# Reordering the start of a hybrid SSD and attention layer: where norms, splits and half steps stand in the queues

## The chip, the cores and the metric

One core of one Trainium2 chip runs the whole layer in one launch. The time is device time in microseconds; a kernel's time is the median of several executions, and one further execution is recorded by the profiler.

## The reference

One decoder layer on a sequence of 1024 tokens with 1024 channels, in float32. RMSNorm, one large projection, a chunked Mamba-2 scan and a forgetting attention side by side, a gated merge, an output projection, a second RMSNorm and the residual:

```python
h = _rmsnorm(x, pre_g)
proj = jnp.einsum('bld,de->ble', h, w_in)
z_ssm, xbc, dt_raw, q, k, v, f_raw, z_att, g_ssm, g_att = jnp.split(proj, ...)
...                       # conv, SiLU, chunked scan -> y_ssm; attention in blocks of 128 -> y_att
p_ssm = jnp.einsum('ble,ed->bld', y_ssm, w_branch_ssm)
p_att = jnp.einsum('ble,ed->bld', y_att, w_branch_att)
merged = jax.nn.sigmoid(g_ssm) * p_ssm + jax.nn.sigmoid(g_att) * p_att
out = jnp.einsum('bld,de->ble', merged, w_out)
return x + _rmsnorm(out, post_g)
```

## The kernel before, in words

The projection's weights are worked off in *pairs* of two units of 128 columns. A pair's product with the normed input is done by a fast 2x2 block scheme with seven block products instead of eight. The operands of the input's side are `b11`, `b21`, `-b22` and the differences `t1`, `-t2`, `t3`, `t4`; those of the weights' side are blocks and sums of blocks (`sum`). Every operand is split into a high part, rounded by ScalarE (`AF.Copy` to fp32r), and a low part, the remainder, made by VectorE. A block product is then 12 matmuls of 128x128 by 128x512: high times high, high times low and low times high, for four blocks of the inner dimension. In the trace the input's operands are called `x0` (`b11`), `x1` (`b21`), `x2` (`-b22`), `x3` (`t1`), `x4` (`-t2`), `x5` (`t3`), `x6` (`t4`), with `h` and `l` for the two parts; the weights' are `wop`.

`Stream` holds the list of block products (*steps*) of all pairs. `stream.halves(n)` issues n half steps of six matmuls each. The list begins with pair 0's product 1, pair 1's product 1, then 0's 2, 1's 2, 0's 6, 5, 7, 4, 3, then pair 1's 6, 5, 7. Three steps ahead of a product its weights are split (`prepare`, lines 349 and 350), and as soon as all readers of a weight buffer are listed, the next load of raw weights (line 342) is queued on SP. Products 1, 6, 7 and 4 of a pair add onto one PSUM bank (`pb`); after 1, 6 and 7 ScalarE copies the bank to `s` (`keep`, line 402). Products 5 and 3 add onto another bank (`pc`); between them line 417 subtracts `s` from it to give a result, on which a tanh follows (line 629).

The start of the kernel is written out in one block. Eight tiles `xt` of x, 128 tokens each, are loaded in two halves. `norm_tiles` computes a tile's sum of squares (line 1197 on ScalarE, for tiles 1 and 3 line 1195 on VectorE), its root (1198, ScalarE), the reciprocal (1199, VectorE), and scales the tile: the first half's on VectorE (1201), the second half's on GpSimd (1203). `stream.begin()` loads more weights and splits those of the first three steps. A loop over k transposes the first half (`turned`, TensorE, line 131, tile `pt`), evicts it with the norm's gain (`low`, lines 1228 and 1230) and splits it into `b11` and `b21` (`put`, lines 1213, 1215, 1217). From k = 4 on each round issues a half step.

A second loop, over j, transposes and evicts the second half (`up`, line 1248), adds to `df`, forms the differences `t1` (1254) and `t2` (1257), splits them, issues a half step and forms `t3` and `t4` in place. Behind it `t3`, `t4` and `-b22` are split, four pieces each, with half steps between; `order=pin` keeps a piece behind what stands before it on its engine. Then the next section opens with its constants (`onesr`, `summing`, `cst`, lines 1288 to 1306), whose generator `dt_and_f` issues the transposing products `pt_df` and goes on with half steps between its parts.

The order on an engine's queue is otherwise chosen by a scheduler at build time: it takes what is ready by its own estimate of times, earlier lines first; instructions under `tc.high_priority()` go ahead of others that are ready. `tc.issue_after(ins)` queues what the block issues on `ins`'s engine behind `ins`, without a wait for its result. TensorE's instructions are kept in the order of the text. On the chip each queue runs strictly in order.

Of the kernel before, what the change touches and what calls it, by code (L numbers as in the profile page):

```python
# [11 lines left out]
AF = mybir.ActivationFunctionType  # L12
ALU = mybir.AluOpType
# [5 lines left out]
D = 1024  # L19
NK = D // P  # L20
KH = NK // 2
# [65 lines left out]
def hybrid_layer(ctx: ExitStack, tc, a, out):  # L87

    nc = tc.nc
# [12 lines left out]
    epst = const.tile([P, 1], F32, name="epst")  # L102
# [24 lines left out]
    def mm(*args, **kw):  # L127
        return tc.keep_in_program_order(nc.tensor.matmul(*args, **kw))  # L128

    def turn(out_, in_, idn=ident):  # L130
        return tc.keep_in_program_order(nc.tensor.transpose(out_, in_, idn))  # L131

    def pin(op):
        return tc.keep_in_program_order(op)

    def small(name="th"):
        return gp.tile([P, HALF], F32, tag="th", name=name)
# [14 lines left out]
    def place(pool, name):  # L152
        i = XOPS.index(name)
        return tuple(pool.tile([P, KH, HALF], F32R, tag=f"x{i}{part}", name=f"x{i}{part}") for part in "hl")
# [4 lines left out]
    class Operands:  # L159
# [37 lines left out]
        def differences(self, j, x, other, cols=slice(0, HALF), room=2, third=None):  # L197
# [48 lines left out]

            wait = (None,) * room
            yield from (start, *wait, less("t1", "x", "x", "y"), keep("b22"), *wait)
            yield from (*low("b22"), less("t2", "x", "y", "x"), keep("b11"), *wait)
            yield from (less("t3", "y", "x", "y"), keep(), *low("t3"), *wait[1:], lambda: fetch("b21"), *wait)  # L250
            yield from (less("t4", "x", "x", "y"), keep(), *low("t4"))

# [34 lines left out]
        def put(self, j, **parts):  # L287
            for name, raw in parts.items():
                self.made.add((name, j))
                name = "-" + name if name in ("t2", "b22") else name  # L290
                self.at[name, j] = self.step
                self.split(name, j, raw)
# [27 lines left out]
    class Pair:  # L320
# [78 lines left out]
        def keep(self, ps):  # L399
            s = wp.tile([P, HALF], F32, tag="s", bufs=3, name="s")  # L400
            with tc.high_priority():
                nc.scalar.activation(s, ps, AF.Copy)  # L402
            return s

        def give(self, unit, ch, ps, s=None, how=None):
# [640 lines left out]
    order = [p for ps in by_group for p in ps]  # L1046
# [120 lines left out]
    with tc.tile_pool(name="pro", bufs=1, reuse_waits="tile", side="right") as pro, tc.tile_pool(  # L1167
        name="prop", bufs=1, space=PSUM, reuse_waits="tile", side="right"
    ) as prop:
        wdf = pro.tile([P, NK, 32], F32, name="wdf")  # L1170
        nc.scalar.dma_start(wdf, a["wdf"])
        preg = pro.tile([P, NK], F32, name="preg")
        nc.scalar.dma_start(preg, a["cst"][:, 80:88])
        ss = pro.tile([P, NT], F32, name="ss")
        rstd = pro.tile([P, NT], F32, name="rstd")
        low = pro.tile([P, NK, HALF], F32, name="low")

        df = prop.tile([P, HALF], F32, name="df")

        early = ExitStack()  # L1180
        xe = early.enter_context(tc.tile_pool(name="xe", bufs=1, reuse_waits="tile"))

        def load_tiles(hf):
            tiles = []
            for t in range(4 * hf, 4 * hf + 4):
                xt = (pro if t < 6 else xe).tile([P, D], F32, tag="xt", bufs=6 if t < 6 else 2, name="xt")
                nc.sync.dma_start(xt, a["x"][t * P : (t + 1) * P, :])
                tiles.append(xt)
            return tiles

        def norm_tiles(hf, tiles):
            for t, xt in enumerate(tiles, 4 * hf):
                sqt = small("sqt").bitcast(BF16)
                if t in (1, 3):
                    nc.vector.tensor_tensor_reduce(sqt, xt, xt, 1.0, 0.0, ALU.mult, ALU.add, ss[:, t : t + 1])
                else:
                    nc.scalar.activation(sqt, xt, AF.Square, accum_out=ss[:, t : t + 1])
                nc.scalar.activation(rstd[:, t : t + 1], ss[:, t : t + 1], AF.Sqrt, bias=epst, scale=1.0 / D)
                nc.vector.reciprocal(rstd[:, t : t + 1], rstd[:, t : t + 1])
                if hf == 0:  # L1200
                    nc.vector.tensor_scalar(xt, xt, rstd[:, t : t + 1], None, ALU.mult)
                else:
                    nc.gpsimd.tensor_scalar(xt, xt, rstd[:, t : t + 1], None, ALU.mult)

        def turned(tiles, k):
            pt = prop.tile([P, HALF], F32, tag="pt", bufs=2, name="pt")
            for j in range(4):
                turn(pt[:, j * P : (j + 1) * P], tiles[j][:, k * P : (k + 1) * P]) 
            return pt

        def put(name, j, src, sign=1.0, order=lambda op: op):
            h, l = (p[:, j, :] for p in xop[name])
            made = [order(nc.scalar.activation(h, src, AF.Copy, scale=sign))]
            if sign == 1.0:
                made.append(order(nc.vector.tensor_tensor(l, src, h, ALU.subtract)))
            else:
                made.append(order(nc.vector.scalar_tensor_tensor(l, src, sign, h, ALU.mult, ALU.subtract)))
            return [op.ins for op in made]

        tiles = load_tiles(0)  # L1220
        stream = Stream(order + late + ends, len(order) + 3, len(order) + len(late) + 4)
        norm_tiles(0, tiles)
        tiles2 = load_tiles(1)
        stream.begin()
        for k in range(NK):
            pt = turned(tiles, k)
            if k > 1:
                nc.scalar.activation(low[:, k, :], pt, AF.Copy, scale=preg[:, k : k + 1])
            else:
                nc.vector.tensor_scalar(low[:, k, :], pt, preg[:, k : k + 1], None, ALU.mult)  # L1230
            put("b11" if k < KH else "b21", k % KH, low[:, k, :])
            if k >= KH:
                stream.halves(1)
        norm_tiles(1, tiles2)

        for k, h in [(k, h) for j in range(KH) for k, h in ((j, 0), (j + KH, 0), (j + KH, 1))]:
            pin(nc.sync.dma_start(wo_dram[k, :, half(h)], a["wo"][k * P : (k + 1) * P, half(h)]))

        b22 = []
        for j in range(KH):  # L1240
            up = []
            if j % 2 == 0:
                two = pro.tile([P, D], F32, tag="xt", bufs=6, name="b22")
                b22 += [two[:, 0:HALF], two[:, HALF:D]]
            for k in (j, j + KH):
                pt = turned(tiles2, k)
                up.append(b22[j] if k >= KH else pro.tile([P, HALF], F32, tag="up", bufs=1, name="up"))
                nc.scalar.activation(up[-1], pt, AF.Copy, scale=preg[:, k : k + 1])
            b11, b21 = low[:, j, :], low[:, j + KH, :]
            for n, (k, m) in enumerate(((j, b11), (j, up[0]), (j + KH, b21), (j + KH, up[1]))):  # L1250
                mm(df[32 * n : 32 * n + 32, :], wdf[:, k, :], m, start=(j == 0), stop=(j == KH - 1))
            with tc.high_priority():
                t1 = small()
                nc.vector.tensor_tensor(t1, up[0], b11, ALU.subtract)
                put("t1", j, t1)
                t2 = small()
                nc.vector.tensor_tensor(t2, up[1], t1, ALU.subtract)
                last = put("-t2", j, t2, -1.0)
            stream.halves(1)

            with tc.issue_after(last[1]) if j == KH - 1 else nullcontext():
                nc.vector.tensor_tensor(b11, t2, b11, ALU.subtract)
                nc.vector.tensor_tensor(b21, t2, b21, ALU.subtract)
        dft = small("dft")
        nc.scalar.activation(dft, df, AF.Identity, bias=bdf)
        stream.halves(1)

        with tc.issue_after(last[0]), tc.issue_after(last[1]):
            for j in range(KH):
                put("t3", j, low[:, j, :], order=pin)  # L1270
        stream.halves(1)
        early.close()
        pools["t4"] = phase_a.enter_context(tc.tile_pool(name="xp4", bufs=1, reuse_waits="tile"))
        xop["t4"] = place(pools["t4"], "t4")
        for j in range(KH):
            put("t4", j, low[:, j + KH, :], order=pin)
        stream.halves(1)
        for j in range(KH):
            put("-b22", j, b22[j], -1.0, order=pin)
        stream.halves(5)  # L1280


    with tc.tile_pool(name="ssm", bufs=1, reuse_waits="tile", side="right") as sp, tc.tile_pool(
# [509 lines left out]
```

## Time and profile before

| | us |
|---|---|
| median of 3 runs | 1277.48 (1276.88 to 1279.33) |
| the profiled execution | 1273.87 |
| its span | 1272.2 |
| TensorE busy | 1246.1 (98%) |
| VectorE busy | 1012.9 (80%) |
| ScalarE busy | 794.3 (62%) |
| GpSimd busy | 319.3 (25%) |

A row of the timeline reads: start, duration, engine, line, operation, output<-inputs, shapes, count, and in brackets the idle time before it and what ended that. SPq is SP's queue, on which transfers are issued. A row with a count above 1 merges instructions that follow each other. L349 and L350 are a weight operand's two halves, L1213 with L1215 or L1217 an input operand's. The last instructions of a product overlap with the next, so a product's length is read from the starts.

### The profile page before, as it was taken

How to read it: one execution, taken by the hardware profiler on the slowest of the kernel's cores; microseconds unless marked ns; L12 is line 12 of the kernel's file. 1: busy time of each engine (PE TensorE's matmuls, PEld its weight loads, DVE VectorE, ACT ScalarE, POOL GpSimd, SP SyncE). 2: the span in 40 equal slices, each digit the busy share in tenths (PEclk: the TensorE clock that was granted, in tenths of full speed). 3: DMA queues.
4: the chain of work that ended last, by engine and by line, in shares of the span. 5: the costliest groups of instructions: out<-in, count | busy, mean ns of one | idle time of the engine just before them, and what ended most of it. 6: DMA issues, size and time to landing. Idle time of an engine off the chain costs nothing.

```text
span 1272.2 us, 20822 instructions
## 1 busy us (share of the span) xinstructions
PE 1246.1 (98%) x6926; PEld 982.3 (77%) x6926; DVE 1012.9 (80%) x1994; ACT 794.3 (62%) x1737; POOL 319.3 (25%) x322
## 2 busy tenths in 40 slices
PE   5999999999999999999999999999999999999997
PEld 3678888888888888888887777777777777778886
DVE  7988886988888978997767676767789767886975
ACT  7745665556665765566555666666687666844753
POOL 4000440013400241115102124223112212356062
PEclk9999999999999999999999999999999999999999
DMA  8232452545436533744447576666687657766933
GB/s 300 69 120 76 146 162 88 191 152 182 138 101 215 175 127 117 219 146 140 142 149 252 162 228 212 217 214 218 232 286 263 224 184 249 249 221 199 364 110 105
DMA packets 152236, 233.56 MB, mean 184 GB/s; under 512 B 15201, under 2 KB 60737, under 8 KB 152129
## 3 DMA queue, kind: packets, MB, share of 16 engines
q1 hardware_dynamic: 136064, 196.08, 47.7%
q10 hardware_dynamic: 10560, 18.06, 3.8%
q0 software_dynamic: 5504, 18.09, 3.7%
q8 instruction: 54, 0.88, 0.3%
q14 instruction: 54, 0.43, 0.1%
HBM read 162.99 MB, written 72.34 MB: 185 GB/s over the span
## 4 chain that ended last, share of the span: by engine, by line
PE 86%; DMA 4%; DVE 4%; ACT 4%; issue 1%; SPq 0%; POOL 0%; DVEq 0%; ACTq 0%; POOLq 0%
PE pb L128 36%; PE pc L128 21%; PE pd L128 7%; PE av L128 5%; PE pt L131 5%; PE s L128 5%; PE yps L128 2%; PE st L128 1%; ACT ex L1509 1%; DMA xt<-in_x 1%; PE tr L131 1%; PE tr_v L131 1%; DMA v<-v_dram 1%; PE df L128 1%; DVE wop L350 1%
## 5 line engine op out<-in xcount | busy, mean ns | idle before, releaser
L350 DVE TENSOR_TENSOR wop<-sum,wop 128x512 fp32r<-128x512 f32 x180 | 140.2, 780 | 53.6 <-ACT wop L349 52.6
L349 ACT ACTIVATE wop<-sum 128x512 fp32r<-128x512 f32 x180 | 112.5, 626 | 109.0 <-DVE sum L355 52.4
L1509 ACT ACTIVATE ex<-ex,nm 128x512 f32<-128x512 f32 (+1 forms) x192 | 116.2, 606 | 71.9 <-DVE nm L1505 71.6
L402 ACT ACTIVATE s<-pb 128x512 f32<-128x512 f32 x144 | 85.3, 593 | 98.2 <-PE pb L128 96.2
L128 PE MATMUL pb<-x0h,wop 128*128 128x512 f32 x384 | 131.5, 399 | 0.0
L128 PE MATMUL pb<-x6h,wop 128*128 128x512 f32 x384 | 129.5, 395 | 1.3 <-ACT s L402 1.3
L128 PE MATMUL pb<-x5h,wop 128*128 128x512 f32 x384 | 130.1, 396 | 0.7 <-ACT s L402 0.7
L350 DVE TENSOR_TENSOR wop<-raw,wop 128x512 fp32r<-128x512 f32 x144 | 105.4, 733 | 31.8 <-ACT wop L349 31.5
L128 PE MATMUL pc<-x3h,wop 128*128 128x512 f32 x384 | 129.8, 396 | 0.5 <-DVE ot L419 0.4
L128 PE MATMUL pc<-x2h,wop 128*128 128x512 f32 x384 | 130.2, 397 | 0.0
L128 PE MATMUL pb<-x4h,wop 128*128 128x512 f32 x384 | 129.1, 395 | 0.0
L1505 DVE CUSTOM_DVE_ANT_0 ex<-s,fb 128x512 f32<-128x512 f32 (+1 forms) x192 | 96.8, 552 | 20.0 <-PE s L128 14.8
L349 ACT ACTIVATE wop<-raw 128x512 fp32r<-128x512 f32 x144 | 89.7, 623 | 14.7 <-PE pd L128 6.1
L128 PE MATMUL pd<-x1h,wop 128*128 128x512 f32 x288 | 96.3, 394 | 0.0
L128 PEld LDWEIGHTS pb<-x6h,wop 128*128 128x128 f32 x384 | 72.1, 188 | 18.6 <-issue 2.0
L128 PEld LDWEIGHTS pb<-x5h,wop 128*128 128x128 f32 x384 | 72.1, 188 | 18.4 <-issue 2.0
L128 PEld LDWEIGHTS pb<-x0h,wop 128*128 128x128 f32 x384 | 72.6, 189 | 17.6 <-issue 2.9
L128 PEld LDWEIGHTS pc<-x3h,wop 128*128 128x128 f32 x384 | 72.1, 188 | 17.7 <-issue 1.5
L128 PEld LDWEIGHTS pc<-x2h,wop 128*128 128x128 f32 x384 | 72.1, 188 | 17.4 <-issue 2.4
L128 PEld LDWEIGHTS pb<-x4h,wop 128*128 128x128 f32 x384 | 72.1, 188 | 16.7 <-issue 1.9
L211 POOL TENSOR_TENSOR wd<-wd 128x256 f32<-128x256 f32 x32 | 32.4, 1011 | 205.0 <-DMA wd<-in_wo 135.0
L131 PE MATMUL pt<-ident,ex 128*128 128x128 f32 x576 | 75.1, 273 | 2.0 <-ACT ex L1509 1.4
(318 smaller groups left out, 2993.6 us busy)
## 6 DMA issues: line engine op xcount, KB each, us to landing
raw<-in_wu SPq DMA_DIRECT2D x128, 256.0 KB
csb<-cs_dram SPq DMA_DIRECT2D x32, 256.0 KB
q<-q_dram SPq DMA_DIRECT2D x32, 256.0 KB
k<-k_dram SPq DMA_DIRECT2D x16, 512.0 KB
fb<-f_dram SPq DMA_DIRECT2D x16, 512.0 KB
rb<-st_dram SPq DMA_DIRECT2D x48, 128.0 KB
wd<-in_wo SPq DMA_DIRECT2D x40, 128.0 KB
xt<-in_x SPq DMA_DIRECT2D x8, 512.0 KB
```

What stands on the lines that cost most here:

```text
L128: return tc.keep_in_program_order(nc.tensor.matmul(*args, **kw))
L131: return tc.keep_in_program_order(nc.tensor.transpose(out_, in_, idn))
L211: pin(nc.gpsimd.tensor_tensor(t[out_], t[a_], t[b_], ALU.subtract))
L349: nc.scalar.activation(op[:, 0], src, AF.Copy)
L350: nc.vector.tensor_tensor(op[:, 1], src, op[:, 0], ALU.subtract)
L402: nc.scalar.activation(s, ps, AF.Copy)
L1505: nc.vector.tensor_tensor_reduce(o, s[e][:, 0:w], fb[hp, h][:, e, 0:w], 1.0, 3.0e38, ALU.add, ALU.min, nm)
L1509: pin(nc.scalar.activation(o, o, AF.Exp, scale=-1.0, bias=nm, accum_out=hd.at(hd.sm, i, h, e)))
```

## The change

The first half's norms are issued under high priority, and the splits in `stream.begin()` are queued behind tile 3's root on ScalarE and behind tile 3's scaling on VectorE. Tile 7 is scaled by VectorE instead of GpSimd. In the last round of the second loop `-t2` is split before `t1`. Of the four pieces of `-b22` the last is split two half steps later, behind the copy `s` of pair 0's product 7, and seven half steps instead of five stand between the first pieces of `-b22` and the next section.

```diff
@@ class Pair
         def keep(self, ps):
             s = wp.tile([P, HALF], F32, tag="s", bufs=3, name="s")
             with tc.high_priority():
-                nc.scalar.activation(s, ps, AF.Copy)
+                self.copied = nc.scalar.activation(s, ps, AF.Copy).ins
             return s
@@ norm_tiles
-                nc.scalar.activation(rstd[:, t : t + 1], ss[:, t : t + 1], AF.Sqrt, bias=epst, scale=1.0 / D)
+                root = nc.scalar.activation(rstd[:, t : t + 1], ss[:, t : t + 1], AF.Sqrt, bias=epst, scale=1.0 / D)
                 nc.vector.reciprocal(rstd[:, t : t + 1], rstd[:, t : t + 1])
-                if hf == 0:
-                    nc.vector.tensor_scalar(xt, xt, rstd[:, t : t + 1], None, ALU.mult)
+                if hf == 0 or t == 7:
+                    scaled = nc.vector.tensor_scalar(xt, xt, rstd[:, t : t + 1], None, ALU.mult)
                 else:
                     nc.gpsimd.tensor_scalar(xt, xt, rstd[:, t : t + 1], None, ALU.mult)
+            return root.ins, scaled.ins
@@ the start
-        norm_tiles(0, tiles)
+        with tc.high_priority():
+            root, scaled = norm_tiles(0, tiles)
         tiles2 = load_tiles(1)
-        stream.begin()
+        with tc.issue_after(root), tc.issue_after(scaled):
+            stream.begin()
@@ the second loop
                 nc.vector.tensor_tensor(t1, up[0], b11, ALU.subtract)
-                put("t1", j, t1)
+                if j < KH - 1:
+                    put("t1", j, t1)
                 t2 = small()
                 nc.vector.tensor_tensor(t2, up[1], t1, ALU.subtract)
                 last = put("-t2", j, t2, -1.0)
+                if j == KH - 1:
+                    with tc.issue_after(last[0]), tc.issue_after(last[1]):
+                        put("t1", j, t1)
             stream.halves(1)
@@ behind it
         stream.halves(1)
-        for j in range(KH):
+        for j in range(KH - 1):
             put("-b22", j, b22[j], -1.0, order=pin)
-        stream.halves(5)
+        stream.halves(3)
+        with tc.issue_after(stream.pairs[0].copied):
+            put("-b22", KH - 1, b22[KH - 1], -1.0, order=pin)
+        stream.halves(4)
```

## The prediction

> **What bounds the kernel now.** I read the page first, then the busy time by stretches, then TensorE's waits, then the timelines of the stretches that wait. Beside the page's share for TensorE stand the stretches (columns: span, TensorE, weight load, VectorE, ScalarE, GpSimd busy, then granted clock, DMA share, GB/s).
>
> ```profile
> PE 1246.1 (98%) x6926; PEld 982.3 (77%) x6926; DVE 1012.9 (80%) x1994; ACT 794.3 (62%) x1737; POOL 319.3 (25%) x322
> 0.00:64.00 64.00, 48.43 (x217) 32.50 (x218) 53.51 (x98) 47.68 (x90) 15.02 (x12) 1.00 0.52 185
> 64.00:200.00 136.00, 136.00 (x720) 109.69 (x719) 117.05 (x213) 80.02 (x163) 28.51 (x24) 1.00 0.42 124
> 12.00:29.00 17.00, 14.17 (x65) 10.47 (x66) 14.85 (x23) 16.96 (x35) 12.89 (x4) 1.00 0.91 323
> 29.00:45.40 16.40, 16.40 (x78) 8.69 (x79) 14.96 (x25) 11.04 (x17) 0.00 (x0) 1.00 0.12 41
> 51.50:55.60 4.10, 2.86 (x13) 2.05 (x11) 4.10 (x8) 4.10 (x8) 0.00 (x0) 1.00 0.60 208
> ```
>
> TensorE is idle for 26.1 us of the span, and 15.6 of them lie in the first 64 us. In the next 136 us it never waits. All edits lie in the first 64 us, so what TensorE gains there it should keep: a fully busy TensorE afterwards just runs the same list earlier. The wait list of TensorE there (total us, times, longest) is the budget:
>
> ```profile
> PE pt L131 <- DVE rstd L1199: 8.6, 1, 8.6
> PE pt L131 <- DVE xt L1201: 2.8, 3, 1.5
> PE pt L131 <- ACT low L1228: 1.4, 1, 1.4
> PE pb L128 <- ACT s L402: 1.3, 1, 1.3
> PE pt L131 <- POOL xt L1203: 0.6, 1, 0.6
> PE pt_df L128 <- DVE summing L1304: 0.5, 1, 0.5
> PE pb L128 <- DVE x4l L1217: 0.3, 1, 0.3
> ```
>
> The first is the start-up and stays. Everything else is 6.9 us, 0.54% of the span: an upper end for any gain. But three stretches have another engine full: ScalarE from 12 to 29 (16.96 of 17.00), TensorE from 29 to 45.4, and both VectorE and ScalarE from 51.5 to 55.6 (4.10 of 4.10 each). A wait that is removed in such a stretch comes back as a wait for the full engine. I call pair 0's seven products p1 to p7, pair 1's q1 to q7.
>
> **Part 1: first half's norms ahead of the weights' split.**
>
> ```profile
> 10.06 0.63 ACT L349 ACTIVATE wop<-raw 128x512 fp32r<-128x512 f32 x1 [0.81 <-DMA raw<-in_wu]
> 10.61 0.29 ACT L1198 ACTIVATE rstd<-ss,epst 128x1 f32<-128x1 f32 x1
> 11.16 0.69 DVE L350 TENSOR_TENSOR wop<-raw,wop 128x512 fp32r<-128x512 f32 x1
> 11.76 0.16 DVE L1199 RECIPROCAL rstd<-rstd 128x1 f32<-128x1 f32 x1
> 12.01 1.06 ACT L1197 ACTIVATE sqt<-xt 128x1024 bf16<-128x1024 f32 x1 [1.11 <-DMA xt<-in_x]
> ```
>
> Tile 3's root ends at 10.90, but its reciprocal stands behind the split and runs at 11.76. With the split behind, it can run at 11.16: tile 3, and the transposes that need it, come 0.6 us sooner. The split's ScalarE half moves from 10.06 to about 10.90, still ahead of the 12.01 at which ScalarE becomes full, and is covered by that idle time. What does 0.6 us bring? From 12 to 29 ScalarE has 0.04 us to spare, and its work (squares, evictions, splits) is the same in both kernels, so the stretch ends where it ended. I take 0. Bounds: -0.6 if it all came through, +0.5 if the split's 0.63 us fell into the full stretch. The raw weights' loads stand on SP's queue as before, since the order is imposed on ScalarE and VectorE alone.
>
> **Part 2: the last tile scaled by VectorE.**
>
> ```profile
> 22.98 0.15 DVE L1199 RECIPROCAL rstd<-rstd 128x1 f32<-128x1 f32 x1
> 24.24 2.85 POOL L1203 TENSOR_SCALAR xt<-xt,rstd 128x1024 f32<-128x1024 f32 x1
> 24.66 1.24 DVE L350 TENSOR_TENSOR wop<-sum,wop 128x512 fp32r<-128x512 f32 x1 [0.34 <-ACT wop L349]
> 27.70 0.64 ACT L349 ACTIVATE wop<-sum 128x512 fp32r<-128x512 f32 x1
> 28.22 0.70 ACT L1248 ACTIVATE up<-pt,preg 128x512 f32<-128x512 f32 x1
> 11.95 0.75 DVE L1201 TENSOR_SCALAR xt<-xt,rstd 128x1024 f32<-128x1024 f32 x1
> ```
>
> Tile 7 is ready at 27.09 now (24.24 + 2.85). On VectorE the same operation costs 0.75 us (the row of tile 3), so it could be ready by 23.13 + 0.75 = 23.9, and TensorE's 0.6 us wait goes. What is late next is the eviction `up` at 28.22, behind ScalarE's unbroken queue. Only one thing ahead of it can give way: p5's split at 27.70, which is traced after `up` and went first. If they swap, `up` starts 0.52 us sooner; if not, nothing is won. I take -0.35, bounds 0 and -0.6. VectorE pays 0.75 and gets back some of it: the split at 24.66, begun just after GpSimd's last scaling, took 1.24 instead of 0.69 us. The net of 0.2 us lies beside TensorE's full stretch from 29 to 45.4, in which VectorE has 1.44 us to spare.
>
> The Trainium skill ("SBUF — State Buffer", Who interferes with whom) speaks against this edit: VectorE and GpSimd share a port pair that one of them locks for a whole instruction, and a scaling on VectorE contends for it. By it the scaling would wait from 23.13 to 24.24 for GpSimd's third tile, 1.1 us more; if VectorE's spare time covered none of that, the sum below would be -0.5 instead of -1.6. The stretched split shows a hold of 0.55 us, not one of 2.85, so the trace agrees with a hold but not with its length.
>
> **Part 3: the last piece of -t2 ahead of t1's.**
>
> ```profile
> 46.23 0.69 DVE L1215 TENSOR_TENSOR x3l<-th,x3h 128x512 fp32r<-128x512 f32 x1
> 47.43 0.69 DVE L1217 SCALAR_TENSOR_TENSOR x4l<-th,x4h 128x512 fp32r<-128x512 f32 x1
> 48.17 0.50 PE L128 MATMUL pb<-x4l,wop 128*128 128x512 f32 x1 [0.30 <-DVE x4l L1217]
> ```
>
> VectorE splits t1 at 46.23 and -t2 at 47.43, and p6 waits 0.30 us for the latter. Swapped, x4l is 0.6 us sooner and the wait goes; t1's piece is needed only by p5's last quarter. What is late next is `s` (part 4), which ScalarE's queue sets, so by itself this brings 0. It may cost: t1's ScalarE half can no longer run ahead of -t2's. Bounds -0.3 and +0.5.
>
> **Part 4: the last piece of -b22 behind the copy `s`.**
>
> ```profile
> 53.47 1.68 ACT L1213 ACTIVATE x2h<-b 128x512 fp32r<-128x512 f32 x3
> 55.03 0.59 ACT L402 ACTIVATE s<-pb 128x512 f32<-128x512 f32 x1
> 55.67 0.50 PE L128 MATMUL pb<-x6h,wop 128*128 128x512 f32 x1 [1.31 <-ACT s L402]
> ```
>
> p4 adds onto the bank that `s` copies, so it cannot start before. Three pieces run from 53.47 to 55.03, 0.52 each; with one behind `s`, p4 starts at 55.15. Bounds: 0 (part 3 gives it back) and -1.3 (the whole wait). The moved piece now also stands behind the tanh of the next result on ScalarE, and behind it pair 1's splits: that chain must be done before p3's last quarter.
>
> **Part 5: two more half steps (p3) before the next section.** They bring p3 ahead of the transposes pt_df, and p3's two loads and q7's split ahead of the section's set-up in the text.
>
> ```profile
> 57.06 0.68 DVE L355 TENSOR_TENSOR sum<-sum,raw 128x512 f32<-128x512 f32 x1
> 57.67 0.69 DVE L1217 SCALAR_TENSOR_TENSOR x2l<-b,x2h 128x512 fp32r<-128x512 f32 x1
> 58.27 0.69 DVE L417 TENSOR_TENSOR th<-pc,s 128x512 f32<-128x512 f32 x1
> 59.23 1.10 PE L128 MATMUL pt_df<-summing,dft 128*128 128x64 f32 x8 [0.53 <-DVE summing L1304]
> 60.14 0.48 PE L128 MATMUL pc<-x2h,wop 128*128 128x512 f32 x1
> 62.97 0.69 DVE L350 TENSOR_TENSOR wop<-sum,wop 128x512 fp32r<-128x512 f32 x1 [0.37 <-ACT wop L349]
> 62.98 0.39 PE L128 MATMUL pb<-x4h,wop 128*128 128x512 f32 x1
> 53.12 0.42 SPq L1296 DMA_DIRECT2D cst<-in_cst  x1
> 61.30 0.33 SPq L342 DMA_DIRECT2D raw<-in_wu  x1
> 63.14 2.72 PE pb L128 x12
> ```
>
> A product takes 2.72 us (the chain's row), pt_df 0.91 (59.23 to 60.14). With parts 2 and 4, p4 runs from 54.8 to 57.5. p3 may follow at once, without the 0.53 us for `summing`, but it writes the bank that the subtraction at 58.27 reads, so that is late next. It loses one 0.60 us piece ahead of it (57.67) and gains part 2's 0.35: 57.3 to 58.0. If the sum at 57.06 also falls behind it, it ends at 57.4 and p4's end, 57.5, decides. So p3 starts between 57.5 and 58.0, and q6, which starts at 62.98 now, between 57.5 + 2.72 + 0.91 = 61.1 and 61.6: a gain of 1.4 to 1.9. On SP's queue p3's loads (61.30, when their buffers come free) are now traced ahead of the constants `cst` (53.12). Nothing ties `cst` to them, so I take 0; issued right behind them it would be 8.5 us late, and its first readers, on VectorE and ScalarE, would wait: that belongs to the backlog below. After q6 the order is the old one. I take the middle, **-1.6 us for all parts together**.
>
> The profiled execution took 1273.87 us, of which 1272.2 are the span; it would become 1272.3. The median shown, 1277.48, is 3.6 above it, so the work is a difference: 1277.48 - 1.6 = **1275.9 us**. One measurement can tell about 0.2%, 2.6 us, from no change; my forecast is inside.
>
> **Rivals.**
> *Free queues (-3.1).* An earlier start makes the schedule put `s` and the subtraction at 58.27 ahead of more pieces than the last one. Then p4 starts without the 1.3 and 0.3 us: 55.67 - 1.6 - 0.5 = 53.6, and p4, p3, pt_df run on: q6 at 59.9. For it: both are marked urgent, and part 3 makes p7 end sooner. Against: VectorE and ScalarE are full there. It gives 1274.4.
>
> *Backlog on VectorE (+1.4).* `summing` is now traced after q6's, q5's and q7's splits, on an engine that is full. If it falls behind q7's split (62.97 + 0.69, less 0.35), pt_df runs from 63.4 and q6 starts at 64.4: 1278.9. It decides as soon as `summing` is later than p3's end, 60.7; each further operation ahead of it costs 0.6, so two more bring +2.6, and a late `cst` more. Against: before, `summing` found a gap ahead of those splits, and can again.
>
> *Nothing (0).* ScalarE's order stays, part 3 eats part 4, and `summing` stalls p3's successor as it stalled p3: 1277.5.
>
> **How the numbers follow.** Forecast 0.43, free queues 0.34, backlog 0.18 (0.14 of it beyond +2.6, since an overfull VectorE tends to hold several operations), nothing 0.05. Faster by over 0.2%: free queues and the forecast's lower edge, 0.35. Within: 0.42 + 0.05 + 0.04 = 0.51. Slower: 0.14. The range goes from 1273.3 (free queues, less 1.1, about half of the 2.45 us over which the three runs of before spread) to 1279.0 (backlog as priced); beyond it I leave 0.2.
>
> **What would show it.** Right: tile 7's scaling on VectorE near 0.75 us with no wait of TensorE for GpSimd; no wait for x4l; `s` directly after three pieces of x2h; p3 right behind p4 and pt_df behind p3 without a wait; q6 at 61.1 to 61.6; no new wait of TensorE from 64 to 600. Wrong: `up` still behind p5's split, a new wait of pt_df for `summing` or of p3 for x2l, or waits that appear past 64 us, where nothing was edited.

## The result and the profile after

The changed kernel took 1280.18 us (median of 19 executions, 1278.09 the lowest) against 1276.88 us for the kernel before (19 executions, beside it on the same chips). The ratio is 1.0028, with a 95% interval of 1.0020 to 1.0036: by the ratio 3.6 us slower, where 1.6 us faster was forecast. One execution of the changed kernel took 3399 us; like single ones of 2067 and 6167 us in later runs, it is left out of the ratios. The profiled execution of after took 1278.09 us, its span 1276.4. First its busy shares and stretches, with the columns as in the prediction:

```profile
PE 1247.9 (98%) x6926; PEld 982.7 (77%) x6926; DVE 1012.1 (79%) x1995; ACT 795.8 (62%) x1738; POOL 312.1 (24%) x321
```

```profile
0.00:64.00 64.00, 47.25 (x201) 30.08 (x201) 49.76 (x88) 46.99 (x87) 9.57 (x9) 1.00 0.48 171
29.00:45.40 16.40, 14.32 (x66) 7.20 (x66) 13.00 (x21) 9.78 (x17) 0.00 (x0) 1.00 0.14 47
```

TensorE did the same 6926 matmuls, but 201 instead of 217 of them in the first 64 us. ScalarE has one instruction more (1738). The stretch from 29 to 45.4, in which TensorE never waited before, now has 2.1 us of idle time. TensorE's waits (total us, times, longest) from 0 to 64 and, in the last two rows, from 64 to 200:

```profile
PE pt L131 <- DVE rstd L1199: 9.0, 1, 9.0
...
PE pb L128 <- ACT s L402: 1.9, 1, 1.9
PE df L128 <- ACT b L1251: 1.5, 1, 1.5
PE pb L128 <- DVE x0l L1216: 0.9, 1, 0.9
...
PE df L128 <- ACT up L1251: 0.6, 1, 0.6
...
PE pc L128 <- ACT x2h L1214: 0.3, 1, 0.3
PE pc L128 <- DVE x2l L1218: 0.2, 1, 0.2
```

The three waits that parts 2, 3 and 5 aimed at are gone: GpSimd's tile (0.6), `x4l` (0.3), `summing` (0.5). In their place stand `b` (1.5), `x0l` (0.9), `up` (0.6), a longer `s` (1.9 for 1.3), `x2h` and `x2l`.

From the timelines of both kernels I take, for one and the same matmul, how much later it starts after the change; I call this its *lag*. The first transpose has +0.39, the first matmul on `up` (28.97 before) +0.67, the fifth such matmul (37.95) +1.20, the second matmul of the next product, p6, (45.66) +3.16, p4 +3.15, q6 +3.39. From there up to 670 us it stays within 0.3 us, for matmuls that keep their place in the order. One 0.8 us wait for a result of line 415 at 675 us and small drifts bring it to +4.2 at the end, which is the difference of the two profiled executions (1278.09 - 1273.87). So most of the loss, 2.5 of 3.4 us, was made between 28 and 45 us, where the change edits nothing.

### The profile page after: what moved, and what is told of

Same layout as the page of the kernel before. It is cut to its first block, busy times and chain, and to the rows that moved or that the text cites. A ratio compares the mean times of both kernels' runs of the same rounds, so it can differ in the third digit from the quotient of the medians.

```text
span 1276.4 us, 20823 instructions
## 1 busy us (share of the span) xinstructions
PE 1247.9 (98%) x6926; PEld 982.7 (77%) x6926; DVE 1012.1 (79%) x1995; ACT 795.8 (62%) x1738; POOL 312.1 (24%) x321
## 4 chain that ended last, share of the span: by engine, by line
PE 84%; DVE 5%; ACT 5%; DMA 4%; issue 1%; SPq 0%; POOL 0%; DVEq 0%; ACTq 0%; POOLq 0%
PE pb L128 36%; PE pc L128 21%; PE pd L128 7%; PE av L128 4%; PE s L128 4%; PE pt L131 4%; PE yps L128 2%; ACT ex L1519 1%; PE st L128 1%; PE tr L131 1%; PE tr_v L131 1%; DVE ex L1515 1%; DVE wop L350 1%; PE tr L128 1%; ACT wop L349 1%
```

## The experiments

Each run stood beside the kernel before on one chip, with 12 executions (6 of two_behind and all_mended). "q6" is the lag of q6's first matmul (62.98 us before) in the profiled execution. The last column turns the ratio into time at 1276.9 us.

| run | ratio, 95% | q6, us | time, us |
|---|---|---|---|
| the whole change | 1.0028 [1.0020, 1.0036] | +3.39 | +3.6 |
| part1_alone | 1.0004 [0.9993, 1.0015] | +1.51 | +0.5 |
| part2_alone | 1.0025 [1.0013, 1.0037] | +2.68 | +3.2 |
| part3_alone | 1.0005 [0.9995, 1.0016] | +1.42 | +0.6 |
| part45_alone | 1.0024 [1.0005, 1.0043] | +1.53 | +3.1 |
| part2_tanh_behind | 1.0003 [0.9992, 1.0014] | +0.67 | +0.4 |
| after_tanh_behind | 1.0012 [1.0003, 1.0022] | +1.39 | +1.5 |
| part45_unpinned | 0.9991 [0.9982, 1.0000] | +0.15 | -1.1 |
| after_no_priority | 1.0025 [1.0011, 1.0039] | +2.97 | +3.2 |
| part5_alone | 1.0000 [0.9989, 1.0010] | -0.45 | 0.0 |
| two_behind | 1.0049 [1.0032, 1.0066] | -1.91 | +6.3 |
| all_mended | 1.0050 [1.0033, 1.0067] | -1.05 | +6.4 |
| four_mended | 1.0005 [0.9993, 1.0017] | -0.08 | +0.6 |

Two cautions for this table. The times of the parts alone add up to 7.4 us and not to 3.6, so no part's share of the loss can be read from it as it stands. And the times hold something that "q6" does not: the granted clock, the share of its full speed that TensorE was given, as the mean over an execution. Where 62 executions of the kernel before had a clock of 0.999, they took 1275.6 us on average; seven with 0.997 took 1279.4. The mean clock was 0.9985 to 0.9987 for the kernel before, 0.9972 in part3_alone, 0.9970 in part45_alone, 0.9962 in all_mended and 0.9957 in two_behind. As an estimate, 0.001 of some 1277 us is 1.3 us, so that about 2 us of part45_alone's +3.1 lie there, more than 3 us in all_mended and almost 4 us of two_behind's +6.3. The main loss is not of that kind: among executions with 0.999 the whole change took 1279.5 us on average (seven) and part2_alone 1278.8 (five), against the 1275.6 of before.

My theory after the result was that each part costs by the order it gives to *other* work in the engines' queues. The main rival was that the edited operations themselves cost: the scaling on VectorE, or the crowded VectorE that the prediction's backlog describes.

**Part 2 alone, and with the tanh tied.**

```diff
-                if hf == 0:
+                if hf == 0 or t == 7:
```

> The kernel before with part 2 alone: tile 7 scaled by VectorE. Theory (queue order): the tanh of pair 0's first result, with its table load of 1.28 us, goes ahead of the second eviction `b` in the third round of the second loop; TensorE waits about 1.5 us for `b` where it waited for nothing, and everything behind it is 2.0 to 2.5 us later: q6 near 65.2, total +2.2. Rival 1 (port lock): the scaling on VectorE takes 1.8 us or more instead of 0.75, and that is the loss: total 0 to +0.5, tanh where it was. Rival 2 (the prediction): -0.35.

The largest loss of a part alone is here: +3.2 us for a single condition. ScalarE in the third round of the second loop, first before, then the whole change:

```profile
37.23 0.67 ACT L1248 ACTIVATE up<-pt,preg 128x512 f32<-128x512 f32 x1
37.80 0.68 ACT L1248 ACTIVATE b<-pt,preg 128x512 f32<-128x512 f32 x1
38.50 1.28 ACT L629 ACT_TABLE_LOAD   x1
39.79 0.63 ACT L629 ACTIVATE th<-th 128x512 f32<-128x512 f32 x1
```

```profile
24.97 0.74 DVE L1201 TENSOR_SCALAR xt<-xt,rstd 128x1024 f32<-128x1024 f32 x1
28.39 0.62 ACT L349 ACTIVATE wop<-sum 128x512 fp32r<-128x512 f32 x1
28.91 0.68 ACT L1251 ACTIVATE up<-pt,preg 128x512 f32<-128x512 f32 x1
...
37.92 0.61 ACT L1214 ACTIVATE x4h<-th 128x512 fp32r<-128x512 f32 x1
38.44 0.67 ACT L1251 ACTIVATE up<-pt,preg 128x512 f32<-128x512 f32 x1
39.12 1.28 ACT L629 ACT_TABLE_LOAD   x1
40.42 0.63 ACT L629 ACTIVATE th<-th 128x512 f32<-128x512 f32 x1
40.95 0.67 ACT L1251 ACTIVATE b<-pt,preg 128x512 f32<-128x512 f32 x1
...
41.68 1.05 PE L128 MATMUL df<-b,wdf 128*32 128x512 f32 x2 [1.47 <-ACT b L1251]
```

Before, `b` stands ahead of the first tanh and of the table load that it brings. After, the order is `x4h`, `up`, table load, tanh, `b`. The table load and the tanh's 0.53 us step (40.42 to 40.95) put 1.8 us ahead of `b`, and TensorE waits 1.47 us for it. part2_alone has the same order (`up` 37.94, table load 38.63, tanh 39.92, `b` 40.46) and the same wait. Why the scheduler chose this order, no run shows. The scaling itself did what the prediction said, 0.74 us on VectorE; in part2_alone it took 1.03. In the next run the tanh is tied behind `b`:

```diff
-            nc.scalar.activation(t[ch], t[ch], AF.Tanh, scale=0.5)
+            def go(order=None):
+                with tc.issue_after(order) if order else nullcontext():
+                    nc.scalar.activation(t[ch], t[ch], AF.Tanh, scale=0.5)
...
+            if stream.count < 6:
+                stream.after(2, lambda: go(stream.evicted))
```

> Part 2 alone, and in addition the tanh of pair 0's first result queued behind the eviction `b` of the third round (nothing else moved). Theory (the loss of part 2 is that queue order): TensorE's wait of 1.5 us for `b` goes, the second loop runs as before, and the lag at q6 falls from 2.6 us to 0.7 us or less; time against before between -0.5 and +0.8 us, where part 2 alone had +3.2. Rival 1 (the loss is the scaling on VectorE itself, by the port it shares with GpSimd): lag at q6 stays at 2 us or more. Rival 2 (the loss lies behind the first 64 us): the wait goes and the time stays at +2.5.

The wait for `b` is gone, and the time is back to 1.0003. The same tie in the whole change:

> The changed kernel whole, and in addition the tanh queued behind the eviction `b`. Theory: the largest single loss goes, lag at q6 from 3.4 to about 1.0 to 1.5 us (what is left is the first table load, the later `s` and the wait for x2h); time against before +0.5 to +1.5 us, ratio near 1.0008, where the change had 1.0028. Rival (the other three parts cost as much by themselves, the sum of the single lags at q6 being 7 us and not 3.4): the time stays at +2.5 or more.

It took 2.0 us off the lag of q6 (3.39 to 1.39) and 2.0 us off the time (+3.6 to +1.5, rounded). This order is the largest single term, shown by taking it out twice.

**Part 1 alone, and the whole change without its priority.** The first has only the priority and the two `issue_after`; the second leaves out `with tc.high_priority()` and keeps the rest.

> The kernel before with part 1 alone: the first half's norms under high priority, the first splits behind tile 3's root and scaling. Theory (a changed queue order costs more than the freed wait): high priority lets the first Square go ahead of the warm-up Sqrt, so ScalarE loads two tables (2 x 1.28 us) where it loaded one; the first transpose comes 0.4 us later, `up` of the second loop 0.5 to 0.7 us later, and pair 1's product 6 (q6, 62.98 before) starts near 63.6: total +0.6. Rival 1 (the prediction: ScalarE is full from 12 to 29, so nothing moves): 0 within 0.3. Rival 2 (the loss of the whole change sits behind the first 64 us): 0 at q6 and a new wait of TensorE later.

> The changed kernel whole, without the high priority around the first half's norms (the split still stands behind tile 3's root and scaling). Theory: ScalarE loads one table at the start again, the first transpose is 0.4 us earlier than in the changed kernel, but the order of squares and evictions behind it is the same, so `up` and all behind it are 0.1 to 0.4 us earlier: ratio to before 1.0025. Rival (the extra table load is the main loss): ratio 1.0010 or less.

ScalarE's start after the whole change:

```profile
2.19 1.28 ACT L1197 ACT_TABLE_LOAD   x1 [2.19 <-issue]
...
6.14 1.28 ACT L105 ACT_TABLE_LOAD   x1
```

The priority let the first square go ahead of the warm-up root, so a function of another table came first, and ScalarE loads two tables instead of one. The Trainium skill ("ScalarE: Activation LUTs", Table sets: the hidden batching unit) says that tables are loaded as sets of functions, and that going from a function of one set to one of another takes a load each time. The trace agrees: here the second load, 1.28 us, came in with the new order. Without the priority there is one load, and the first transpose has a lag of -0.08 instead of +0.39. But q6 changed only from +3.39 to +2.97, and the time (1.0025 against 1.0028) can't tell. part1_alone shows a lag of +1.51, with waits for `x0l` (1.2) and `x0h` (0.8), since squares and evictions changed places on the full ScalarE. But part of this lag is not the order's: behind these waits TensorE ran at half clock from 22.5 to 25.9 us, which it did not in the profile of the whole change (granted clock third from the end):

```profile
24.00:26.00 2.00, 2.00 (x7) 1.61 (x7) 2.00 (x4) 1.97 (x5) 1.68 (x1) 0.52 0.82 281
```

Its time of 1.0004 holds both that and nothing. So the extra load is shown in the trace; its share of the time stays unsettled.

**Part 3 alone.**

```diff
+                if j < KH - 1:
+                    put("t1", j, t1)
...
+                if j == KH - 1:
+                    with tc.issue_after(last[0]), tc.issue_after(last[1]):
+                        put("t1", j, t1)
```

> The kernel before with part 3 alone: the last piece of -t2 split ahead of t1's. Theory (queue order): the wait of 0.3 us for x4l goes, p5 and p7 start 0.5 us sooner, but the copy `s` now stands behind dft and the last piece of x6h on ScalarE, so p4 starts where it did or 0.2 us later: total 0 to +0.2. Rival (the wait was all there was): p4 and all behind it 0.3 to 0.5 us sooner, total -0.4.

The wait for `x4l` went, and the wait for `s` grew from 1.31 to 2.38. p7 ended 0.46 us sooner, and `s` came 0.62 us later (55.65 for 55.03); I had expected p4 at most 0.2 us later, and its lag grew by 0.5. My expectation blamed `dft` and the last `x6h`, but both stood ahead of this `s` before too (`dft` at 48.76). ScalarE has no gap from 45.7 up to `s`, and only one instruction there is new: `t1`'s half `x3h`. Before, it ran at 43.45, ahead of a gap; now it takes 0.52 us of the full stretch. So here the cost is the moved piece's own place, and not an order given to other work. First before, then part3_alone:

```profile
43.45 0.63 ACT L1213 ACTIVATE x3h<-th 128x512 fp32r<-128x512 f32 x1
45.62 0.63 ACT L349 ACTIVATE wop<-raw 128x512 fp32r<-128x512 f32 x1 [1.54 <-PE pd L128]
```

```profile
46.77 0.61 ACT L1213 ACTIVATE x3h<-th 128x512 fp32r<-128x512 f32 x1
...
54.56 0.68 ACT L1269 ACTIVATE dft<-df,bdf 128x512 f32<-128x512 f32 x1
...
55.65 0.58 ACT L402 ACTIVATE s<-pb 128x512 f32<-128x512 f32 x1
...
56.29 0.50 PE L128 MATMUL pb<-x6h,wop 128*128 128x512 f32 x1 [2.38 <-ACT s L402]
```

The whole change shows the same thing. `x3h` stands in the full stretch, at 49.85, and takes the place that part 4 freed, so that part 4's gain is gone:

```profile
49.85 0.61 ACT L1214 ACTIVATE x3h<-th 128x512 fp32r<-128x512 f32 x1
...
55.54 1.67 ACT L1214 ACTIVATE x2h<-b 128x512 fp32r<-128x512 f32 x3
...
58.20 0.57 ACT L402 ACTIVATE s<-pb 128x512 f32<-128x512 f32 x1
58.83 0.50 PE L128 MATMUL pb<-x6h,wop 128*128 128x512 f32 x1 [1.86 <-ACT s L402]
...
61.01 1.15 ACT L349 ACTIVATE wop<-sum 128x512 fp32r<-128x512 f32 x2 [2.24 <-DVE sum L355]
61.70 0.43 PE L128 MATMUL pc<-x2h,wop 128*128 128x512 f32 x1
...
62.07 0.58 ACT L413 ACTIVATE th<-pb 128x512 f32<-128x512 f32 x1
62.55 1.14 ACT L629 ACTIVATE th<-th 128x512 f32<-128x512 f32 x2
63.59 0.62 ACT L1214 ACTIVATE x2h<-b 128x512 fp32r<-128x512 f32 x1
...
64.26 0.50 PE L128 MATMUL pc<-x2h,wop 128*128 128x512 f32 x1 [0.28 <-ACT x2h L1214]
```

The same rows show part 5's price. p3 starts right behind p4 at 61.70, as meant, but its last quarter needs the moved piece of `x2h`. That stands pinned behind two splits, a copy and two tanh and runs at 63.59. With its low part and the two waits p3 takes 3.86 us (61.70 to pt_df at 65.56) instead of the 2.72 of the prediction.

**Parts 4 and 5 alone, pinned and not pinned.**

```diff
-        for j in range(KH):
+        for j in range(KH - 1):
...
+        with tc.issue_after(stream.pairs[0].copied):
+            put("-b22", KH - 1, b22[KH - 1], -1.0, order=pin)
```

> The kernel before with parts 4 and 5 alone: the last piece of -b22 behind the copy `s`, and two more half steps ahead of the next section. Theory (queue order): `s` is 0.5 us sooner and p4 with it; p3 follows p4 at once, but the last x2h stands behind the tanh and two weight splits on ScalarE, so p3 waits 0.5 to 1.0 us in its last quarter; q6 0.5 us sooner (62.5), total -0.5. Rival 1 (the prediction's parts 4 and 5 without part 2): q6 1.0 to 1.5 us sooner, total -1.3. Rival 2 (constants queued behind weight loads on SP stall VectorE and TensorE later): +0.8 or more, with the wait past 64 us.

> Parts 4 and 5 alone, but the last piece of -b22 tied only to the copy `s` and no longer to what stands ahead of it in the text, so that it runs on ScalarE right behind `s`, ahead of the tanh and the weights' splits. Theory (p3's waits of 1.2 and 0.2 us come from that place in the queue): both go, p3 runs through, and q6 starts 1.0 to 2.0 us earlier than before instead of 1.5 later; time against before -1.0 to -2.0 us. Rival (the constants queued behind weight loads on SP are the loss of parts 4 and 5): the waits for x2h go and the time is still above before by 1 us or more.

Pinned, `s` came 0.45 us sooner, as the prediction has it, and p3 then waited 1.2 us for `x2h` and 0.2 for `x2l`: q6 at +1.53, where I had expected -0.5. Its time of +3.1 is more than this order, since about 2 us go with the lower clock; its three executions with a clock of 0.999 took 1275.5 us on average, no more than before. Whether the order brought the lower clock stays open. In the second run only `order=pin` of the last piece is left out. ScalarE then takes that piece right behind `s`:

```profile
55.53 0.58 ACT L402 ACTIVATE s<-pb 128x512 f32<-128x512 f32 x1
56.01 0.63 ACT L1213 ACTIVATE x2h<-b 128x512 fp32r<-128x512 f32 x1
```

p3's waits for `x2h` and `x2l` are gone. Its q6 lag of +0.15 includes +1.0 us that it already had at 28.97 us, ahead of all that was edited (matmuls start 0.43 us apart up to 23.6 us there, up to 20.2 us before), so the edit itself brought about -0.9; I had expected -1.0 to -2.0. Its time, 0.9991 [0.9982, 1.0000], is the only one of these runs with an interval that does not reach above 1, and that only just. It is the best version found, some 1.1 us below before and, by the two ratios, 4.7 us below the change.

**Part 5 alone**: `halves(7)` for `halves(5)`, all four pieces ahead of `s`.

> Part 5 alone: seven half steps instead of five behind the pieces of -b22, all four of which stay ahead of the copy `s`. Theory (the waits for x2h come from the moved piece, not from the moved half steps): no wait for x2h or x2l; p4 starts as before (wait for `s` 1.3 us), p3 follows within 0.4 us of p4's end once the subtraction of L417 is done, pt_df has no wait; q6 0.5 to 0.9 us earlier than before; time -0.3 to -1.0 us. Rival (the constants, queued behind weight loads on SP, stall VectorE and ScalarE): time above before by 0.5 us or more, with a wait of TensorE past 64 us.

q6 comes 0.45 us sooner and the time is 1.0000, where I had expected a gain of 0.3 to 1.0 us. In its profile later waits of 1.5 us for `x3l`, 0.6 for line 417 and 0.5 for line 415 took the place of what was won.

**Two pieces and `dft` behind `s`, without parts 1 and 2, and then with all five parts.**

```diff
-        nc.scalar.activation(dft, df, AF.Identity, bias=bdf)
...
+        with tc.issue_after(stream.pairs[0].copied):
+            nc.scalar.activation(dft, df, AF.Identity, bias=bdf)
+            for j in range(KH - 2, KH):
+                put("-b22", j, b22[j], -1.0)
```

> Parts 3, 4 and 5 with the orders mended: -t2 ahead of t1, two pieces of -b22 (not one) and dft behind the copy `s`, tied to `s` alone; part 1 and part 2 left out. Theory (each wait comes from what stands ahead on ScalarE): `s` loses dft and two pieces ahead of it, p4 starts 1.0 to 1.3 us earlier than before, no wait for x4l, x2h or x2l, q6 1.3 to 1.8 us earlier; time against before -1.5 to -2.2 us, better than parts 4 and 5 unpinned (-1.2). Rival (VectorE is full there and takes the place of ScalarE: the subtraction of L417 ends when it did): p3 waits 0.5 us or more for L417, q6 no earlier than 0.8 us before, time -0.8 or less.

> All five parts with the four orders mended: no high priority for the norms, tanh behind the eviction `b`, two pieces of -b22 and dft behind `s` and tied to it alone. Theory: what is left of parts 1 and 2 costs 0.3 to 0.8 us at the second loop (`up` later, since squares and evictions change places on a full ScalarE), the rest gains 1.5: time against before -0.5 to -1.2 us, worse than the same without parts 1 and 2. Rival (once the orders are mended parts 1 and 2 bring what the prediction gave them): better than without them, -2.0 us or more.

My expectation held up to 64 us and failed behind it. q6 came 1.91 us sooner, the best of all runs, and the kernel was 6.3 us slower. The wait that took over in two_behind; the timeline of two_behind, with the exponential that stands in the chain behind this wait (ScalarE) and the chain's last step (VectorE); and the same two rows before:

```profile
PE pt_te L128 <- DVE da L716: 4.8, 1, 4.8
```

```profile
65.55 0.40 ACT L693 ACTIVATE t<-t 128x256 f32<-128x256 f32 x1
...
90.22 0.28 DVE L716 SCALAR_TENSOR_TENSOR da<-dtn,ea 128x128 f32<-128x128 f32 x1
```

```profile
62.84 0.40 ACT L693 ACTIVATE t<-t 128x256 f32<-128x256 f32 x1
...
83.84 0.28 DVE L716 SCALAR_TENSOR_TENSOR da<-dtn,ea 128x128 f32<-128x128 f32 x1
```

The step sizes' chain is a long row of small steps, each in a gap between large splits on VectorE. Before, its last step ended at 84.12, and pt_te needs it at 84.74. Its exponential 2.7 us later (65.55), behind three splits and a copy on ScalarE, became 6.4 us at its end. The wait alone would leave the kernel some 2.9 us behind (4.8 - 1.9). Behind it TensorE ran at half clock up to 95.4 us (third from the end), and the lag went from about +3.0 to +5.5 at 110 us. all_mended waits for `da` just as long. The half clock in two_behind:

```profile
90.60:95.40 4.80, 4.75 (x17) 3.56 (x18) 0.00 (x0) 1.20 (x4) 0.00 (x0) 0.50 0.01 3
```

That such a chain stood only 0.6 us ahead of its reader was to be read in the trace of before; no wait marks it there.

**Parts 1, 2, 4 and 5 with the blamed orders taken out**: no priority, the tanh tied, the last piece not pinned; part 3 left undone.

> Parts 1, 2, 4 and 5 with the three orders taken out that the traces blame: part 1 without the high priority (the split only imposed behind the norms), the tanh of the second loop's third round queued behind `b`, and the last piece of -b22 tied to `s` but otherwise free in its queue. Part 3 is left undone, since alone it traded one wait for another and with parts 4 and 5 it moved the exponential of the step-size chain. My theory, that each part costs by the order that it gives to queued work elsewhere and not by its own operations: one table load of 1.28 us at the start, no wait of TensorE for `b` over 0.3 us, none for x2h or x2l in p3, the 0.3 us wait for x4l still there, exponential of the chain not later than before, no wait of pt_te above 1 us, q6 0.5 to 1.2 us earlier than before (62.98), and a time of -0.3 to -1.5 us against before: a ratio of 0.9988 to 0.9998. Rival 1, that the operations themselves cost (tile 7's scaling on VectorE, the splits moved behind the norms): q6 later than before by 0.5 us or more, ratio 1.001 or above although those orders are gone. Rival 2, that any earlier p3 runs into the serial chain behind it: q6 earlier, but pt_te waits 2 us or more and the ratio is 1.002 or above.

```profile
PE pb L128 <- ACT s L402: 0.7, 1, 0.7
PE df L128 <- ACT up L1257: 0.6, 1, 0.6
PE pb L128 <- DVE x0l L1223: 0.4, 1, 0.4
PE pb L128 <- DVE x4l L1225: 0.3, 1, 0.3
PE pc L128 <- DVE th L417: 0.2, 1, 0.2
```

The waits for `b`, `x2h` and `x2l` are gone, and there is none from 64 to 200. q6 stands at -0.08 and the time at 1.0005 [0.9993, 1.0017]: the loss of 3.6 us is gone, within what can be told. The gain is not there. I expected q6 at least 0.5 us sooner and a ratio of 0.9998 or less. The lag at 45.66 us is still +0.81 (+0.29 at the first `up`, and +0.52 where `x4h` goes ahead of `up` in the third round, as in the whole change), and parts 4 and 5 bring it down by 0.89. Neither rival fits.

## Why the prediction was wrong

**The step that failed first** is in part 2: "What is late next is the eviction `up` at 28.22", with the bounds 0 and -0.6. `up` did stay behind p5's split (28.91 behind 28.39), which the prediction named as the case without a gain. But the scheduler worked out all of ScalarE's later order anew, and ten microseconds further on a tanh with its table load went ahead of `b`. That cost 2.0 us, and no part of the sum had a place for it: the sum put what the new order does further on at nothing. For most parts I asked what is late next *in the old order*.

**Part 1** was to be 0, because ScalarE's work "is the same in both kernels". The order in the full stretch changed, and 1.28 us of table load came on top ahead of it (6.14). Tile 3 did come sooner: the transposes at 12.76 have a lag of -0.31, and -0.69 without the priority, where 0.6 was predicted. Behind the wait for `x0l` (0.9) the lag was +0.8, and without the wait for tile 7 close to 0 again, until the wait for `up` (0.6). The lag at the first matmul on `up` is +0.67 with part 2 beside it and +0.30 without the priority; the bound was +0.5. In part1_alone it is +1.19, with the half clock in it.

**Part 2's** own operation was right: 0.74 us, no wait for GpSimd. The port rule cited there was not put to the test in the whole change, for GpSimd's three scalings ended at 23.77 (14.74 + 9.03), 1.2 us before VectorE's began. In part2_alone they did meet: GpSimd's third ran from 19.99 to 23.84, and VectorE's took 0.3 us more than its 0.75. To wait for the third's end would have taken 0.5, but GpSimd's times are rough, so this decides little:

```profile
23.37 1.03 DVE L1201 TENSOR_SCALAR xt<-xt,rstd 128x1024 f32<-128x1024 f32 x1
```

In part2_tanh_behind they missed each other, and the scaling took 0.75.

**Part 3** at 0 was right in kind: the wait went over to `s`. Alone TensorE waited 1.1 us more there (2.38 for 1.31), and won only the 0.3 us of `x4l`; p4's lag grew by 0.52 (from +0.09 to +0.61), the upper bound, and through `t1`'s ScalarE half, which could no longer run ahead of `-t2`'s, as the prediction feared.

**Part 4** was right where it stood alone (p4 -0.45, predicted -0.52). In the whole change part 3's `x3h` used it up, which was its bound of 0.

**Part 5** was right in its structure: p3 directly behind p4, no wait of pt_df, the old order behind q6. It failed at a condition that part 4 states, "that chain must be done before p3's last quarter". I wrote that down and did not price it. The chain was done 1.1 us too late.

**The rivals.** The side of the backlog (+1.4) came true, but not its mechanism. `summing` was on time, and VectorE was no fuller than before. `cst` did fall behind four loads of weights on SP's queue, as that rival feared:

```profile
55.37 9.17 SPq L342 DMA_DIRECT2D raw<-in_wu  x4
64.58 0.44 SPq L1306 DMA_DIRECT2D cst<-in_cst  x1
```

It is issued 11.5 us later than before (53.12), and TensorE did not wait for it. That no new wait would come from 64 to 600 held but for p3's own two. The range ended at 1279.0, the backlog as priced, and so left out what happened: several small losses by order at once.

## What to carry to other kernels

Where a scheduler sets the order of the queues, the cost of an edit is the new order of all that comes behind it. Before moving an operation, list what each engine holds within the next twenty microseconds that must not change places (a table load, an eviction that TensorE reads at once, the head of a serial chain), and tie those first. An earlier product is worth something only if the chains behind it have slack: read from the trace of before how long ahead of its reader each chain ends, since a chain that is just in time shows no wait.

## What the runs showed of the hardware

In part3_alone TensorE's granted clock fell to half about 1 us after a wait of 2.38 us, and for some 3.4 us matmuls started 0.43 us apart instead of 0.23. The stretch from 58 to 60, whose granted clock stands third from the end (the wait ahead of it is the last row of part3_alone above):

```profile
58.00:60.00 2.00, 2.00 (x6) 1.52 (x6) 2.00 (x8) 1.72 (x3) 0.68 (x1) 0.50 0.00 0
```

That added 0.8 to 0.9 us to q6's lag (+0.61 at p4, +1.49 at pt_df). In part1_alone waits of 0.8 and 0.9 us were enough for the half clock from 22.5 to 25.9; in the whole change, a single wait of 0.9 us at the same place was followed by none. A wait of 1.47 us at 1117.8 us in part2_alone was followed by clocks of 0.59 and 0.55 in the next two stretches of 2 us, and one of 1.53 us at the same place in part5_alone by 1.00. So a wait of one to two microseconds can cost about as much again, or nothing. That is a likely reason why executions of one kernel differ by some microseconds (before: 1274.38 to 1280.33): the mean times by granted clock, given under the table of the experiments, go the same way. The Trainium skill ("TensorE: Matmul & The Clock Gate", What's actually happening) puts the return to half speed after at least one idle window of about 3.4 us, which runs freely of the kernel. The run-to-run difference fits a free-running window; that a full idle one is needed does not fit these waits.
